# The beginning of an attention layer: where the context's norm, K's rotation and four scalings stand

## The chip, the cores and the metric

The kernel runs on one core of one Trainium2 chip. The metric is device time in microseconds (us). The program computes a whole two-layer model, and its time is that of one execution.

## The reference, cut to what matters

The model has a latent stream of 1024 tokens, a context of 256 tokens, and a width of 1024. Each layer first normalises and modulates its input, and then mixes. What is touched here is the first part of the first layer, the attention layer:

```
shift, scale, gate = adaln(c, w_ada[0], b_ada[0])              # latent; the context has its own three
u  = rms_normalize(h)  * (1 + scale[:, None]) + shift[:, None]
uc = rms_normalize(hc) * (1 + scale_c) + shift_c
q, k, v, g = split(u @ w_in)       # q 1024, k 256, v 256, g 1024 columns; the same for uc
q, k = axial_rope(q, row, col), axial_rope(k, row, col)        # the latent tokens' alone
...
y = (o * silu(g)) @ w_out
```

## The kernel before, in words

The tokens lie in three tiles, `TT = [(0, 512), (512, 512), (1024, 256)]`: tile 0 and tile 1 are the latent tokens, tile 2 is the context. A tile's activations are held transposed, as eight pieces of 128 features by 512 (or 256) tokens, with an index k of 0 to 7. Every fp32 product is made of three products of rounded halves: a value x is split in a high part (`uH` for activations, `wh` for weights, a cast on ScalarE) and a low part (`uL`, `wl`, the difference, on VectorE or GpSimd), and `mm3` issues high by high (L248 of before), and the two mixed products (L249, L250).

`norm0` prepares the input. For tile 0 it sums the squares, computes the modulation's vectors (`ada0`, from the weights `w_ada`), and has the inner function `modulate(e)`, which does the half e of the eight pieces: it scales and shifts a piece in place (the tile named `uL`, since it lies in the buffer that tile 1's low part takes later), casts it to `uH`, and subtracts for the low part. For e = 0 the scaling is one `tensor_scalar` on VectorE (L469), for e = 1 it is one `activation` on ScalarE (L471). Beside it run four projections of the gate (`half(e, x)`, x from 0 to 3), whose results are taken up by `g_out`: a tanh on ScalarE (L567), a multiplication on VectorE (L568), and a store. Then, in one loop, tiles 1 and 2 are normalised: `stats(i)` squares the rows on ScalarE (L442) and gives the factor per token (`rr`), and `modulate(0, h, r, i, k)` scales a piece on VectorE (L309), casts it on ScalarE (L310) and makes the low part on VectorE (L311). The context's pieces are the tiles `xc`.

`qkvg` then projects. `kproj(x, i)` makes two heads of K for tile i: 24 matrix products into one accumulator, then, for i < 2, the rotation `rope` (multiplication by the cosine L527 and a shuffle `STREAM_SHUFFLE` L528 on VectorE, which are the last two readers of the accumulator, multiplication by the sine on GpSimd L529, an addition on VectorE L530), a cast (L548) and the low part `kL` (L549), a store to DRAM and copies back into `kHH`, issued by GpSimd. `vproj(b)` makes V for 128 tokens: 24 matrix products into an accumulator, a cast (L602), and the low part `v` on VectorE (L603), the last reader of the accumulator. The order of tile 0 is `kproj(0, 0)`, four `vproj`, `kproj(1, 0)`; then tile 1, then tile 2, then Q and the rest of the gate.

The accumulators of all these are tiles of one name, `pj`, of which there are four: a projection can begin when the fourth one before it has been read out. Matters of order: every engine runs its own queue in order. The queues' order comes from a scheduling layer, which follows the order of the code where dependencies and its own estimate leave it, and which `issue_after(x)` tells to hold what is written inside until after instruction x. Memory of a closed pool is taken again by later tiles, which then wait for the last users.

Of the kernel before, what the change touches and what calls it, by code (L numbers as in the profile page):

```python
# [17 lines left out]
P = 128  # L18
D = 1024
KT = D // P  # L20
LAT = 1024
# [92 lines left out]
class Kernel:  # L114
# [203 lines left out]
    def layer0(self):  # L318
        nc, t, a = self.nc, self.t, self.a
        cps = ExitStack()  # L320
        BUFS.update(S=1, pj=4, wr=7, qf=2, ql=2, wh=4, wl=4, sqt=2)
        self.psA = self.pool("psA", space=PSUM, ctx=cps)
        NB = (LAT + CTX) // P
        self.uH, self.uL = [None] * 3, [None] * 3
        cw = ExitStack()
        wvp = self.pool("wv", ctx=cw)

        self.wp = self.pool("wq", ctx=cw)
        self.pq = self.pool("qf", ctx=cw)
# [4 lines left out]
        c0 = ExitStack()  # L334
        self.q_d = [[t(self.dr, [4, 2, HD, n], F32, f"q{j}_{i}") for i, (_, n) in enumerate(TT)] for j in range(KV)]
        self.sg_d = [[t(self.dr, [2, P, n], F32, f"sg{j}_{i}") for i, (_, n) in enumerate(TT)] for j in range(KV)]
        wk, wv = self.norm0(c0, p, wvp)
        c0.close()
        ckv = ExitStack()
        kvp = self.pool("kv", ctx=ckv, side="right")  # L340
        self.kHH = [t(kvp, [P, LAT + CTX], F32R, f"kHH{j}") for j in range(KV)]
# [5 lines left out]
        self.qkvg(p, wk, wv, wvp)  # L347
# [48 lines left out]
        self.modulation(0, n, row, ps)  # L396
        return mm, self.last_mod

    def norm0(self, c0, p, wvp):


        nc, t, a = self.nc, self.t, self.a
        ps = self.psA
        p1 = self.p0 = self.pool("n0", ctx=c0, side="right")
        hs, nat, raws = {}, {}, {}


        xc = [t(p1, [P, KT // 2, CTX], F32, "xc", 2) for _ in range(2)]

        def load_x(i):  # L410

# [25 lines left out]

        def stats(i):

            ss = t(p1, [P, 4], F32, "ss", 2)  # L440
            for b, x in enumerate(nat[i]):
                nc.scalar.activation(x, x, AF.Square, accum_out=ss[:, b : b + 1])  # L442
            return self.rstd_n(p1, ss, TT[i][1], D)
# [10 lines left out]
        acc = t(p1, [P, 512], F32, "sqa")  # L454
        nc.scalar.activation(acc, hs[0][0], AF.Square)
        for k in range(1, KT):
            sq = t(p1, [P, 512], F32, "sqt")
            nc.scalar.activation(sq, hs[0][k], AF.Square)
            nc.vector.tensor_tensor(acc, acc, sq, op=ALU.add)
        r = self.rstd_c(p1, acc, 512, D)  # L460
        self.alloc_u(0)
        m = self.mod[0]
        pj = [t(ps, [P, 512], F32, "pj") for _ in range(G0)]
# [1 line left out]
        def modulate(e):  # L465
            for k in range(4 * e, 4 * e + 4):
                h, uh = hs[0][k], self.uH[0][:, k, :]
                if e == 0:
                    nc.vector.tensor_scalar(out=h, in0=h, scalar1=m[:, 8 + k, 0:1], scalar2=m[:, k, 0:1], op0=ALU.mult, op1=ALU.add)  # L469
                else:  # L470
                    nc.scalar.activation(h, h, AF.Identity, bias=m[:, k, 0:1], scale=m[:, 8 + k, 0:1])  # L471
                nc.scalar.copy(uh, h)  # L472
                nc.vector.tensor_sub(self.uL[0][:, k, :], h, uh)

# [36 lines left out]
        modulate(1)  # L511
        for x in range(G0):
            half(1, x)
            self.g_out(p if x < 2 else p1, pj[x], x, 0, "qf" if x < 2 else "gq")
        for i in (1, 2):
            r = stats(i)
            self.alloc_u(i)
            for k in range(KT):
                self.modulate(0, hs[i][k], r, i, k)
        return wk, wv  # L520

    def rope(self, pool, ps, i, out):
        nc = self.nc
        s, n = TT[i]
        b = self.t(pool, [P, 512], F32, "rope_b")
        s -= self.rope_o
        nc.vector.tensor_mul(out, ps, self.cos[:, s : s + n])  # L527
        nc.vector.stream_shuffle(b, ps, mask=[(j + 16) % 32 for j in range(32)])  # L528
        nc.gpsimd.tensor_tensor(b, b, self.sin[:, s : s + n], op=ALU.mult)  # L529
        nc.vector.tensor_add(out, out, b)  # L530

# [42 lines left out]
    def g_step(self, p, w, x, i):  # L574
        self.g_out(p, self.proj_h(self.psA, w, self.uH, self.uL, i), x, i)

    def qkvg(self, p, wk, wv, wvp):
# [9 lines left out]
        def kproj(x, i):  # L587
            s, n = TT[i]
            h, _ = self.qk(p, self.proj_h(ps, wk[x], self.uH, self.uL, i), i, self.kL[x][:, s : s + n])
            nc.sync.dma_start(kh_d[x][i], h.bitcast(F32))  # L590
            for e in range(2):
                for hf in range(2):
                    nc.gpsimd.dma_start(self.kHH[2 * x + e][hf * HD : (hf + 1) * HD, s : s + n], kh_d[x][i][e * HD : (e + 1) * HD, :])

        def vproj(b):
            i = 0 if b < 4 else (1 if b < 8 else 2)
            o = (b * P) - TT[i][0]
            pj = t(ps, [P, 512], F32, "pj")
            self.mm3(pj[:, :256], [(self.uH[i][:, k, o : o + P], self.uL[i][:, k, o : o + P],
                                    wv[k // 2][0][:, k % 2, :], wv[k // 2][1][:, k % 2, :]) for k in range(KT)])  # L600
            pv = pj[:, :256].rearrange("p (j d) -> p j d", j=KV)
            nc.scalar.copy(v[:, b, :, :HD], pv)  # L602
            nc.vector.tensor_sub(v[:, b, :, HD:], pv, v[:, b, :, :HD])  # L603
# [1104 lines left out]
```

## Time and profile before

| | |
|---|---|
| runs before | 1789.54, 1794.72, 1792.93 us; median 1792.93 |
| profiled execution | 1788.45 us, of which the span of the trace is 1786.8 us |
| instructions | 28991 |
| busy | TensorE (PE) 97%, VectorE (DVE) 67%, ScalarE (ACT) 49%, GpSimd (POOL) 45% |

A profile line gives, for an instruction or a run of like ones, its start in us from the start of the span, its length, its engine, the line of the code, the operation, what it writes and reads, and how many; in square brackets stands the time for which the engine stood idle before it, and what released it. PEld is TensorE's loading of weights, which overlaps the products. PEclk is the clock that TensorE was granted, as a share of the full one.

### The profile page before, as it was taken

Reading aid. Unit: us, or ns where it says so; the run is one execution under the profiler, and the core shown is the slowest. Engines: PE = TensorE matmul, PEld = TensorE weight load, DVE = VectorE, ACT = ScalarE, POOL = GpSimd, SP = SyncE. Lnnn points to the kernel's source line nnn. Section 1 sums busy time; section 2 is a strip of 40 time slices with the busy share of each in tenths; the row PEclk is TensorE's granted clock in tenths of the full one; section 3 lists DMA queues with packets and bytes.
Section 4 is the critical chain, followed back from the end, with each engine's and each line's share of the span. In section 5 each row is a group of like instructions: output and inputs, shape, how many; then the busy total and the mean of one; then the engine's idle time right before and its main releaser. Section 6 shows DMA issues by size and latency. Waiting matters only on the chain.

```text
span 1786.8 us, 28991 instructions
## 1 busy us (share of the span) xinstructions
PE 1733.4 (97%) x10319; PEld 1493.5 (84%) x10319; DVE 1197.2 (67%) x2115; ACT 874.4 (49%) x1906; POOL 799.0 (45%) x1068
## 2 busy tenths in 40 slices
PE   6899999999999999999999999999999999999997
PEld 2697788888888877778898898989889898988887
DVE  4634436778877885685776858677685867876634
ACT  3612227777777774452444534444453444544522
POOL 2431127555575555103555463736446363554321
PEclk9999999999999999999999999999999999999998
DMA  9658866444554536212323323232332322555533
GB/s 346 221 147 267 280 183 152 111 96 106 114 152 129 130 101 221 86 53 74 80 69 89 84 74 93 72 85 75 90 85 72 91 77 81 180 166 167 182 103 114
DMA packets 211931, 227.61 MB, mean 127 GB/s; under 512 B 15820, under 2 KB 149068, under 8 KB 211788
## 3 DMA queue, kind: packets, MB, share of 16 engines
q1 hardware_dynamic: 177724, 207.12, 38.8%
q0 software_dynamic: 34064, 18.65, 5.7%
q8 instruction: 81, 1.33, 0.3%
q14 instruction: 62, 0.51, 0.1%
HBM read 190.88 MB, written 35.13 MB: 126 GB/s over the span
## 4 chain that ended last, share of the span: by engine, by line
PE 84%; DVE 9%; issue 2%; ACT 2%; DMA 2%; POOL 0%; SPq 0%; DVEq 0%; ACTq 0%; POOLq 0%
PE pj L1106 18%; PE pj L1140 10%; PE pj L1541 7%; PE pj L248 7%; PE pj L249 6%; PE pj L250 6%; PE psD L1091 4%; PE psX L1293 3%; PE pt L686 3%; PE psD L1209 2%; PE pv L693 2%; PE psX L1262 2%; PE psX L1261 2%; PE pv L692 2%; PE S L661 1%
## 5 line engine op out<-in xcount | busy, mean ns | idle before, releaser
L248 PE MATMUL pj<-uH,wh 128*128 128x512 f32 (+1 forms) x712 | 257.3, 363 | 6.3 <-ACT uH L472 3.7
L249 PE MATMUL pj<-uL,wh 128*128 128x512 f32 (+1 forms) x712 | 243.3, 342 | 0.5 <-POOL uL L709 0.4
L250 PE MATMUL pj<-uH,wl 128*128 128x512 f32 (+1 forms) x712 | 242.4, 341 | 1.3 <-POOL wl L233 1.1
L1106 PE MATMUL pj<-uH,wh 128*128 128x512 f32 x512 | 173.6, 411 | 1.2 <-ACT bn L1061 1.2
L1106 PE MATMUL pj<-uH,wl 128*128 128x512 f32 x512 | 170.2, 403 | 0.0
L1106 PE MATMUL pj<-uL,wh 128*128 128x512 f32 x512 | 168.1, 402 | 0.0
L1184 POOL TENSOR_TENSOR xw<-xn,dtdec 128x256 f32<-128x256 f32 x144 | 95.9, 667 | 159.8 <-PE psD L1209 75.7
L248 PEld LDWEIGHTS pj<-uH,wh 128*128 128x128 f32 x712 | 135.6, 191 | 34.0 <-issue 6.3
L250 PEld LDWEIGHTS pj<-uH,wl 128*128 128x128 f32 x712 | 135.0, 190 | 18.5 <-POOL wl L233 2.1
L1140 PE MATMUL pj<-wh,uH 128*128 128x256 f32 x512 | 150.4, 294 | 0.0
L1140 PE MATMUL pj<-wl,uH 128*128 128x256 f32 x512 | 150.2, 293 | 0.0
L1140 PE MATMUL pj<-wh,uL 128*128 128x256 f32 x512 | 149.9, 293 | 0.0
L249 PEld LDWEIGHTS pj<-uL,wh 128*128 128x128 f32 x712 | 135.8, 191 | 16.1 <-issue 3.0
L691 DVE TENSOR_TENSOR pl<-pt,ph 128x512 fp32r<-128x512 f32 x168 | 114.1, 688 | 47.2 <-ACT ph L690 46.0
L233 POOL TENSOR_TENSOR wl<-wr,wh 128x512 fp32r<-128x512 f32 x76 | 99.6, 1315 | 85.4 <-ACT wh L231 84.5
L665 DVE CUSTOM_DVE_ANT_0 sm<-S,mask,nsink 128x640 f32<-128x640 f32 (+2 forms) x160 | 119.2, 772 | 19.7 <-PE S L661 12.6
L1325 ACT ACTIVATE uT<-psX,nw 128x128 f32<-128x128 f32 x128 | 46.6, 364 | 171.6 <-PE psX L1324 170.7
L667 ACT ACTIVATE sm<-sm,nm 128x640 f32<-128x640 f32 (+2 forms) x160 | 118.7, 742 | 16.7 <-DVE nm L665 16.1
L690 ACT CAST ph<-pt 128x512 fp32r<-128x512 f32 x168 | 97.5, 585 | 55.8 <-PE pt L686 51.8
L231 ACT CAST wh<-wr 128x512 fp32r<-128x512 f32 (+1 forms) x116 | 74.7, 648 | 87.0 <-PE pj L249 67.1
L1106 PEld LDWEIGHTS pj<-uH,wl 128*128 128x128 f32 x512 | 95.8, 188 | 20.0
L1106 PEld LDWEIGHTS pj<-uL,wh 128*128 128x128 f32 x512 | 95.3, 188 | 19.3
(342 smaller groups left out, 4861.9 us busy)
## 6 DMA issues: line engine op xcount, KB each, us to landing
wr<-w_x SPq DMA_DIRECT2D x32, 512.0 KB, 4.2
M<-acs SPq DMA_DIRECT2D x64, 256.0 KB, 5.3
bw<-acs SPq DMA_DIRECT2D x64, 256.0 KB, 5.7
wr<-w_sk SPq DMA_DIRECT2D x24, 512.0 KB, 4.5
wr<-wg SPq DMA_DIRECT2D x40, 256.0 KB, 4.3
qs<-q POOLq DMA_DIRECT2D x40, 256.0 KB, 3.9
wada<-w_ada SPq DMA_DIRECT2D x16, 512.0 KB, 8.1
wr<-wq SPq DMA_DIRECT2D x32, 256.0 KB, 2.9
```

The source lines that it names most:

```text
L233: (eng or nc.vector).tensor_tensor(l, raw, h, op=ALU.subtract)
L248: self.nc.tensor.matmul(ps, lh, rh, start=first and i == 0, stop=False)
L249: self.nc.tensor.matmul(ps, lh, rl, start=False, stop=False)
L250: self.last_mm = self.nc.tensor.matmul(ps, ll, rh, start=False, stop=last and i == n - 1)
L665: nc.vector.tensor_tensor_reduce(out=sm[:, :W], in0=Sv, in1=self.mask[:, m0 : m0 + W], scale=-SCALE, scalar=self.nsink[:, 4 * j + r : 4 * ...
L667: nc.scalar.activation(sm[:, :W], sm[:, :W], AF.Exp, bias=nm[:, r : r + 1], scale=-1.0, accum_out=sums[:, r : r + 1])
L690: nc.scalar.copy(ph, ptf)
L691: nc.vector.tensor_sub(pl, ptf, ph)
L1106: self.pe = nc.tensor.matmul(raw[:, 512 * i : 512 * i + 512], l[:, k, :], r[i][:, k, :], start=k + y == 0, stop=k == KT - 1 and y == 2)
L1140: self.pe = nc.tensor.matmul(pj[:, c], l, r[:, k, :], start=c % 2 + q + k + y == 0, stop=c % 2 == 1 and q == 1 and k == 3 and y == 2)
L1184: nc.gpsimd.tensor_tensor(xw, X(st, c).rearrange("p (r h) -> p r h", r=R), self.dtdec[:, c, hd(d, g)].unsqueeze(2).broadcast_to([P, R, HP] ...
L1541: self.pe = nc.tensor.matmul(banks[x], l[:, z, sl], r, start=k == 2 * qs[0] and y == 0, stop=k == 2 * qs[-1] + 1 and y == 2)
```

## The change

Four things are changed.

- `norm0` ends after the first half (k = 0 to 3) of tile 1. The other half, and all of tile 2, become a function `late`, which `qkvg` calls: the second half of tile 1 is issued after the shuffle of `kproj(0, 0)`, and tile 2's norm after the last V of tile 0 has been read out.
- `modulate(1)` scales on VectorE, as `modulate(0)` does.
- The fourth gate result of tile 0 (x = 3) goes into a tile of its own, `sqa`, in the place of the third one's `gq`.
- The memory is rearranged for this: the context's tiles are in a pool `n1` that stays open longer, and K's `kHH` is allocated after that pool is closed, so that tile 0's copies into `kHH` (`spread`) are issued then.

```
@@ norm0
-                if e == 0:
-                    nc.vector.tensor_scalar(out=h, in0=h, scalar1=m[:, 8 + k, 0:1], scalar2=m[:, k, 0:1], op0=ALU.mult, op1=ALU.add)
-                else:
-                    nc.scalar.activation(h, h, AF.Identity, bias=m[:, k, 0:1], scale=m[:, 8 + k, 0:1])
+                nc.vector.tensor_scalar(out=h, in0=h, scalar1=m[:, 8 + k, 0:1], scalar2=m[:, k, 0:1], op0=ALU.mult, op1=ALU.add)
...
-            self.g_out(p if x < 2 else p1, pj[x], x, 0, "qf" if x < 2 else "gq")
-        for i in (1, 2):
-            r = stats(i)
-            self.alloc_u(i)
-            for k in range(KT):
-                self.modulate(0, hs[i][k], r, i, k)
-        return wk, wv
+            self.g_out(p if x < 2 else p1, pj[x], x, 0, "qf" if x < 2 else ("gq", "sqa")[x - 2])
+        rs = {}
+
+        def late(i, ks):
+            if i not in rs:
+                rs[i] = stats(i)
+                self.alloc_u(i)
+            for k in ks:
+                self.modulate(0, hs[i][k], rs[i], i, k)
+
+        late(1, range(4))
+        return wk, wv, late
@@ qkvg
-        for i, (s, n) in enumerate(TT):
+        kproj(0, 0)
+        with self.tc.issue_after(self.turned.ins):
+            late(1, range(4, KT))
+        for b in range(4):
+            low = vproj(b)
+        kproj(1, 0)
+        with self.tc.issue_after(low.ins):
+            late(2, range(KT))
+        keys()
+        for x in range(2):
+            spread(x, 0)
+        for i, (s, n) in list(enumerate(TT))[1:]:
             kproj(0, i)
-            if i:
-                kproj(1, i)
+            kproj(1, i)
             for b in range(s // P, (s + n) // P):
                 vproj(b)
-            if i == 0:
-                kproj(1, i)
```

Here `self.turned` is the shuffle that `rope` issued last, `keys()` closes the pool `n1` and allocates `kHH`, and `spread(x, i)` is the four copies into `kHH` that stood in `kproj`.

What the rewriting does to the queues is seen at two places. The first is ScalarE's queue at `modulate(1)`, tile 0's second half. Before, the scalings (L471, on the tile `uL`) stand between casts of weights (`wh`) and ahead of the four casts to `uH`:

```order
L231 CAST wh_144_442<-wvr_143_440 128x512
L471 ACTIVATE uL1_65_164<-uL1_65_164,mod0_5_74 128x512 x2
L231 CAST wh_147_448<-wvr_146_446 128x512
L471 ACTIVATE uL1_65_164<-uL1_65_164,mod0_5_74 128x512 x2
L231 CAST wh_150_454<-wvr_149_452 128x512
L472 CAST uH0_99_244<-uL1_65_164 128x512 x2
L231 CAST wh_135_424<-wr_134_422 128x512
L472 CAST uH0_99_244<-uL1_65_164 128x512
```

Now, in the same place of ScalarE's queue:

```order
L231 CAST wh_144_445<-wvr_143_443 128x512
L231 CAST wh_147_451<-wvr_146_449 128x512
L475 CAST uH0_99_247<-uL1_65_167 128x512
L231 CAST wh_150_457<-wvr_149_455 128x512
L475 CAST uH0_99_247<-uL1_65_167 128x512 x3
L231 CAST wh_135_427<-wr_134_425 128x512
```

And on VectorE, where the scalings (L474 now) stand between the modulation's vector (`mod`) and the four subtractions (L476):

```order
L223 TENSOR_SCALAR mod0_5_74<-mod0_5_74 128x8
L474 TENSOR_SCALAR uL1_65_167<-uL1_65_167,mod0_5_74 128x512 x4
L476 TENSOR_TENSOR uL0_100_248<-uL1_65_167,uH0_99_247 128x512 x4
L385 TENSOR_TENSOR sqt_177_585<-ident_1_63,rc_176_582 128x512
L576 SCALAR_TENSOR_TENSOR qf_171_525<-qf_171_525,pj_101_249 128x512
```

Four scalings have left ScalarE's queue, the first cast to `uH` waits for one scaling in the place of four, and VectorE has all four scalings ahead of the first subtraction.

The second place is VectorE's queue at the accumulators of tile 0: the norm of tile 1 (L309 and L311 on `uH2`, `uL2`, the loaded halves), K's rotation (`rope_b`), the norm of tile 2 (`xc`), the fourth gate (`gq_174`, reading `pj_104`), and the four V (`v`). Before:

```order
L309 SCALAR_TENSOR_TENSOR uL2_166_485<-uL2_166_485,mod0_5_74,rr512_179_586 128x512 x4
L311 SCALAR_TENSOR_TENSOR uL1_181_589<-uH2_165_484,mod0_5_74,uH1_180_588 128x512 x4
L380 TENSOR_TENSOR sqt_184_620<-ident_1_63,rc_183_617 128x256
L311 SCALAR_TENSOR_TENSOR uL1_181_589<-uL2_166_485,mod0_5_74,uH1_180_588 128x512 x4
L527 TENSOR_TENSOR qf_206_700<-pj_205_675,cos_167_488 128x512
L528 STREAM_SHUFFLE rope_b_208_702<-pj_205_675 128x512
L309 SCALAR_TENSOR_TENSOR xc_61_160<-xc_61_160,mod0_5_74,rr512_186_624 128x256 x4
L309 SCALAR_TENSOR_TENSOR xc_62_161<-xc_62_161,mod0_5_74,rr512_186_624 128x256 x4
L568 SCALAR_TENSOR_TENSOR gq_174_570<-gq_174_570,pj_104_249 128x512
```

After (the fourth gate is `sqa_174`):

```order
L576 SCALAR_TENSOR_TENSOR sqa_174_573<-sqa_174_573,pj_104_252 128x512
L309 SCALAR_TENSOR_TENSOR uH2_165_487<-uH2_165_487,mod0_5_74,rr512_179_589 128x512 x4
L311 SCALAR_TENSOR_TENSOR uL1_181_592<-uH2_165_487,mod0_5_74,uH1_180_591 128x512 x4
L535 TENSOR_TENSOR qf_195_649<-pj_194_624,cos_167_491 128x512
L536 STREAM_SHUFFLE rope_b_197_651<-pj_194_624 128x512
L309 SCALAR_TENSOR_TENSOR uL2_166_488<-uL2_166_488,mod0_5_74,rr512_179_589 128x512 x4
L538 TENSOR_TENSOR qf_195_649<-qf_195_649,rope_b_197_651 128x512
L311 SCALAR_TENSOR_TENSOR uL1_181_592<-uL2_166_488,mod0_5_74,uH1_180_591 128x512 x3
L616 TENSOR_TENSOR v_182_609<-pj_198_671,v_182_609 128x4x64
L616 TENSOR_TENSOR v_182_609<-pj_199_698,v_182_609 128x4x64
```

The readers of the accumulators (the fourth gate, the cosine and the shuffle of K, the low parts of V) now stand ahead of the context's norm, and K's first two readers stand ahead of tile 1's second half; the rotation's addition (L538), which waits for GpSimd, stands ahead of the low parts of V.

More of the change, by code (lines that the diff above doesn't have):

```diff
@@ L346, in layer0, with keys @@
         self.sink = t(kvp, [P, HEADS], F32, "sink")
-        self.qkvg(p, wk, wv, wvp)
+        def keys():
+            c2.close()
+            kh = self.pool("kvh", ctx=ckv, side="right")
+            self.kHH = [t(kh, [P, LAT + CTX], F32R, f"kHH{j}") for j in range(KV)]
+        self.qkvg(p, wk, wv, wvp, late, keys)
         if "u" in self.dump:
@@ L404, in norm0 @@
         p1 = self.p0 = self.pool("n0", ctx=c0, side="right")
+        p2 = self.pool("n1", ctx=c2)
         hs, nat, raws = {}, {}, {}
[L408 removed]
+        xc = [t(p2, [P, KT // 2, CTX], F32, "xc", 2) for _ in range(2)]
         def load_x(i):
@@ L527, in rope @@
         nc.vector.tensor_mul(out, ps, self.cos[:, s : s + n])
-        nc.vector.stream_shuffle(b, ps, mask=[(j + 16) % 32 for j in range(32)])
+        self.turned = nc.vector.stream_shuffle(b, ps, mask=[(j + 16) % 32 for j in range(32)])
         nc.gpsimd.tensor_tensor(b, b, self.sin[:, s : s + n], op=ALU.mult)
@@ L575, in g_step, with qkvg @@
         self.g_out(p, self.proj_h(self.psA, w, self.uH, self.uL, i), x, i)
-    def qkvg(self, p, wk, wv, wvp):
+    def qkvg(self, p, wk, wv, wvp, late, keys):
         nc, t, a = self.nc, self.t, self.a
@@ L590, in kproj, with spread @@
             nc.sync.dma_start(kh_d[x][i], h.bitcast(F32))
+            if i:
+                spread(x, i)
+        def spread(x, i):
+            s, n = TT[i]
             for e in range(2):
```

17 lines of the change are left out of this document (8 added, 9 removed).

## The prediction

> **What bounds the kernel now.** I read, in this order, TensorE's (PE's) waits in the stretch around the change, its timeline there, the windows for its clock, and then the queues of the engines it waits for. The waits between 20 and 140 us (engine and line, released by what, total us, times, longest):
>
> ```profile
> PE pj L248 <- ACT uH L472: 3.7, 2, 2.8
> PE pj L248 <- DVE rope_b L528: 2.3, 1, 2.3
> PE pj L248 <- DVE gq L568: 1.6, 1, 1.6
> PE pj L248 <- DVE v L603: 1.6, 1, 1.6
> ```
>
> The first line is the cast of tile 0's second half (its longest case, 2.8; the other lies ahead of the change). The others are the four accumulators `pj`: PE stands because VectorE (DVE) has not yet read one out. PE's timeline shows where these stand in the work:
>
> ```profile
> 52.02 1.65 PE L248 MATMUL pj<-uH,wh 128*128 128x512 f32 x3 [2.77 <-ACT uH L472]
> 53.47 0.73 PE L249 MATMUL pj<-uL,wh 128*128 128x512 f32 x1
> ...
> 55.24 0.39 PE L250 MATMUL pj<-uH,wl 128*128 128x512 f32 x1
> ...
> 65.05 0.79 PE L248 MATMUL pj<-uH,wh 128*128 128x512 f32 x1
> ...
> 70.93 0.28 PE L248 MATMUL pj<-wh,uH 128*128 128x256 f32 x1
> ...
> 77.13 0.28 PE L250 MATMUL pj<-wh,uL 128*128 128x256 f32 x1
> 79.74 0.39 PE L248 MATMUL pj<-wh,uH 128*128 128x256 f32 x1 [2.34 <-DVE rope_b L528]
> ...
> 82.60 0.28 PE L250 MATMUL pj<-wh,uL 128*128 128x256 f32 x1
> 84.51 0.39 PE L248 MATMUL pj<-wh,uH 128*128 128x256 f32 x1 [1.63 <-DVE gq L568]
> ...
> 87.37 0.28 PE L250 MATMUL pj<-wh,uL 128*128 128x256 f32 x1
> 89.22 0.50 PE L248 MATMUL pj<-uH,wh 128*128 128x512 f32 x1 [1.57 <-DVE v L603]
> ```
>
> K's first projection runs from 65.05, the four V from 70.93, K's second head pair begins at 89.22, and two V's first products and that of K are late. Windows of PE's work and clock (us, then per engine busy time and count, then PEclk, the share of the DMA engines, GB/s):
>
> ```profile
> 48.40:51.80 3.40, 0.85 (x4) 0.38 (x2) 0.00 (x0) 3.40 (x6) 1.82 (x3) 1.00 1.04 406
> 51.80:55.20 3.40, 3.18 (x7) 2.34 (x8) 3.20 (x3) 3.40 (x8) 2.41 (x2) 0.50 1.04 418
> 82.50:85.90 3.40, 1.77 (x15) 1.56 (x14) 3.40 (x9) 2.33 (x6) 0.00 (x0) 1.00 0.17 64
> 85.90:89.30 3.40, 1.83 (x16) 1.63 (x14) 3.40 (x9) 1.41 (x5) 1.38 (x3) 1.00 0.52 106
> 89.30:250.00 160.70, 160.70 (x1015) 131.16 (x1016) 64.01 (x120) 37.22 (x72) 33.27 (x40) 1.00 0.73 229
> ```
>
> The last row matters most: from 89.3 to 250 us PE is busy for all of 160.70 us, at full clock. What the change takes from the front is therefore passed on, unless it makes a wait of its own.
>
> **First part: the scalings on VectorE.** Before, the vector `mod` is ready and ScalarE (ACT) scales in two pairs, with casts of weights between:
>
> ```profile
> 46.62 0.84 DVE L223 TENSOR_SCALAR mod<-mod 128x8 f32<-128x8 f32 x1
> 47.49 1.52 ACT L471 ACTIVATE uL<-uL,mod 128x512 f32<-128x512 f32 x2 [0.91 <-DVE mod L223]
> ...
> 49.43 1.51 ACT L471 ACTIVATE uL<-uL,mod 128x512 f32<-128x512 f32 x2
> ```
>
> PE stands for 2.77 us, then does its three high products, then needs the first low part, at 53.47. Now VectorE scales four times, then subtracts. The nearest rows are those of the first half, which already goes that way, beside GpSimd (POOL) making low parts of weights (the line of a source line's view gives nanoseconds, lowest, median, highest):
>
> ```profile
> L469 DVE TENSOR_SCALAR uL<-uL,mod x4: 535/1466/1491, 25.6 to 29.8; 128x512 f32<-128x512 f32 x4
> 25.57 4.72 DVE L469 TENSOR_SCALAR uL<-uL,mod 128x512 f32<-128x512 f32 x4
> 30.21 2.48 DVE L473 TENSOR_TENSOR uL<-uL,uH 128x512 fp32r<-128x512 f32 x4
> 23.27 6.28 POOL L233 TENSOR_TENSOR wl<-wr,wh 128x512 fp32r<-128x512 f32 x4 [6.45 <-ACT wh L231]
> ```
>
> The scaling that falls behind POOL's last operation takes 535 ns, those beside POOL 1466: VectorE waits for POOL. POOL has such low parts to make in the second half too (1.82 us of them in the window from 48.40). I take the whole 4.72: 47.49 + 4.72 = 52.21 for the end of the scalings, and a quarter of 2.48, 0.62, for the first subtraction: 52.8. The first cast to `uH` comes after one scaling, 1.47, so PE does its three high products near 49.6 and then waits again. At 52.8 it needs the low part: 0.6 us earlier than 53.47. VectorE's time is not hidden here; it is what PE waits for. What ScalarE loses, four times about 0.75, was on this path before and is now off it.
>
> The rest of this term is the clock. After the gap the window 51.80 to 55.20 has a clock of 0.50, and from 53.47 to 55.24 four products take 1.77 us; at the pace of K's first projection (65.05 to 70.93, 24 products in 5.88, 0.245 each) they would take 1.0. PE was busy for 0.85 of 3.4 us in the window whose gap cost it the clock, and 1.77 and 1.83 of 3.4 in two that kept it. The change puts three products, some 0.8 us, into the gap: 1.65 of 3.4, nearer to those that kept it. With full clock the gain is 0.6 + 0.8 = 1.4, with the same drop 0.6. I take 1.0, between the two, since the windows' phase need not be that of this execution.
>
> The Trainium skill, "TensorE: Matmul & The Clock Gate", section "Why this matters for your kernels", says that matmul bursts should have no gaps over about 3 us between them, or the clock goes to half. The trace differs a little: a gap of 2.77 us was enough. By that rule both of the change's shorter gaps leave the clock full and the term is 1.4 in the place of 1.0.
>
> Bounds of this term: above, the 535 ns for all four scalings, 47.49 + 2.14 + 0.62 = 50.3, so 3.2 earlier, and 0.8 for the clock: a gain of 4.0. Below, 1491 for each, and for the first subtraction the 1774 that a two-input VectorE operation takes at most beside POOL (row L311 below): 47.49 + 5.96 + 1.77 = 55.2, a loss of 1.8. I stay at 1.0, since the row of 4.72 is the same operation with the same neighbour.
>
> **Second part: who reads the accumulators first.** Rows of VectorE before:
>
> ```profile
> 78.36 0.68 DVE L527 TENSOR_TENSOR qf<-pj,cos 128x512 f32<-128x512 f32 x1
> ...
> 78.97 0.71 DVE L528 STREAM_SHUFFLE rope_b<-pj 128x512 f32<-128x512 f32 x1
> 79.59 4.27 DVE L309 SCALAR_TENSOR_TENSOR xc<-xc,mod,rr 128x256 f32<-128x256 f32 x8
> 83.78 0.67 DVE L568 SCALAR_TENSOR_TENSOR gq<-gq,pj 128x512 f32<-128x512 f32 x1
> ...
> 88.76 1.07 DVE L603 TENSOR_TENSOR v<-pj,v 128x256 fp32r<-128x256 f32 x3
> ```
>
> K's accumulator is full at 70.93 and read at 78.36, behind all of tile 1's norm; the fourth gate's is full before 65.05 and read at 83.78, behind eight scalings of the context; V's low parts come at 88.76, behind the rest of the context. The three stalls, from the end of the last product at its pace of 0.12 to the next start, are 79.74 - 77.25 = 2.49, 84.51 - 82.72 = 1.79, and 89.22 - 87.49 = 1.73: 6.0 us. Where do the readers come now? For this I need
>
> ```profile
> 66.27 2.85 DVE L309 SCALAR_TENSOR_TENSOR uH<-uH,mod,rr 128x512 f32<-128x512 f32 x4 [1.89 <-ACT rr L384]
> 71.69 2.73 DVE L311 SCALAR_TENSOR_TENSOR uL<-uH,mod,uH 128x512 fp32r<-128x512 f32 x4
> L311 DVE SCALAR_TENSOR_TENSOR uL<-uL,mod,uH x4: 737/739/1774, 74.7 to 77.7; 128x512 fp32r<-128x512 f32 x4
> 73.32 0.60 ACT L231 CAST wh<-wvr 128x512 fp32r<-128x512 f32 x1
> 74.00 1.90 POOL L233 TENSOR_TENSOR wl<-wvr,wh 128x512 fp32r<-128x512 f32 x1 [2.34 <-ACT wh L231]
> 79.77 1.44 POOL L529 TENSOR_TENSOR rope_b<-rope_b,sin 128x512 f32<-128x512 f32 x1 [3.86 <-DVE rope_b L528]
> ```
>
> The fourth gate is read right after its tanh, ahead of the row at 66.27: no wait. Tile 1's first half: scaling from 66.27 to 69.1, low parts to 71.8, K's cosine and shuffle to 73.2. The accumulator that K leaves is wanted by the fourth V, near 79: cover of 6 us. The next one needed is that of the first V, by K's second head pair. On PE that is due at 65.05 + 5.88 + 96 products of 0.12 = 82.4. On VectorE: four scalings of the second half, 2.85, to 76.0, and 1.03 for one of them caught by POOL (1774 less 739), 77.0. Then the addition, which waits for the product with the sine. That stands on POOL behind the low part of the last quarter of V's weights, whose cast ACT reaches no later than before, 73.32, since it has four pieces fewer ahead: 73.9, two POOL operations of 1.90 and 1.44, 77.3 (77.5 with the small power operation in the way). Addition 0.68, three low parts 2.2, V's low part 0.36: 80.7. So 1.7 us of cover are left, and if POOL or VectorE is later than that by more, each us costs one. All of tile 1's `uL` is there by 82, and wanted 5.9 after 82.4.
>
> The context's norm, now begun only after K's second pair's shuffle near 89, needs 4.27 for scaling and 2.85 or more for low parts, beside the 23 us that PE has in two K of tile 1 (5.88 each) and four V (2.9 each): it is hidden, and so are tile 0's copies into `kHH`, first read in the attention. GpSimd issues them ahead of tile 1's products with the sine and waits there for the context's last low part, near 97 (89 + 4.27 + 2.85 and a wait or two); what stands behind those products on VectorE are V's low parts of tile 1, whose accumulators PE wants no earlier than its context projections, near 111 (82.4 + 3 times 5.88 + 4 times 2.9). The gate's store in SP's queue passes two loads of Q's weights, which PE wants after all of that. I cost these at nothing.
>
> **The sum.** 6.0 + 1.0 = 7.0 us. Against the profiled execution of 1788.45 that is 1781.4; this execution is 4.5 below the median of the runs, so for the median I subtract from that: 1792.93 - 7.0 = 1785.9. About 0.3%, 5.4 us, is what a measurement of this kernel can tell from no change, so the forecast stands 1.6 us beyond that.
>
> **The rivals.** First, a part is lost: the scalings go by their lower bound (a loss of 1.8 in the place of a gain of 1.0), or the addition is later than its cover and K's second pair waits as long. For it speaks that every VectorE operation met by POOL is stretched (1466 for 535, 1774 for 739); against it, that the cover counts one such meeting already. 6.0 - 1.8 = 4.2, so 1788.7. The Trainium skill, "SBUF — State Buffer", section "SBUF: two separate sides", has the port pair of VectorE and GpSimd as an exclusive lock for a whole instruction; the trace agrees with 535 against 1466, and it is the rule that speaks against putting scalings there.
>
> Second, the 7 us are given back, because a later stretch is set by something else, such as the transfers of Q's weights. For it: the DMA share of 0.73 up to 250. Against it: PE waits there for nothing. 1792.9.
>
> Third, it gets slower. The last quarter of V's weights is loaded late, and now the rotation's addition, and behind it V's low parts, stand in VectorE's queue behind what POOL makes of it, while PE's third and fourth V want it too.
>
> ```profile
> 57.21 0.37 SPq L501 DMA_DIRECT2D wvr<-wv x1
> ...
> DMA to landing us min/median/max: 7.4/7.4/7.4
> ```
>
> Issued at 57.21 behind loads that wait for buffers which POOL frees, it lands near 64.6; its low part (2.5 us later) is wanted by PE near 77.2, so a landing after 74.7 costs each us, and from 81.7 all gain is gone. POOL delayed by scalings could hold SP's queue. Three more landing times, 22 us, would put it at 86.8: 12.1 lost, 1785.9 + 12.1 = 1798.0, 5.1 slower than before. Against it stand 10 us of cover.
>
> **How the numbers follow.** Forecast 0.68, first rival 0.17, second 0.09, third 0.06. The runs shown spread over 5.2 us, so of the forecast some 0.85 is measured beyond 5.4 us, of the first rival 0.3: 0.58 + 0.05 = 0.63 for faster. Slower by over 0.3%: half of the third, and some scatter of the second, 0.06. The rest, 0.31, is the same. Range: the second part alone with the lower bound gives 1788.7, and scatter of 2.8 on it 1791.5; the sum with the first term's upper bound, 10.0, gives 1782.9, and 2.4 of scatter 1780.5. This leaves out most of the second and all of the third rival.
>
> **What would show it.** Right: PE without a wait between K's first projection and 250 us, K's second pair beginning near 81.4, the first subtraction of the second half ending near 52.8, PEclk 1.00 after it. Wrong: a wait of PE for the low part of V or the shuffle (cover too small), scalings that end after 53.5, or a span shorter by 7 us at 250 and not at its end.

## The result, and the profile after

The changed kernel takes 1786.11 us (median of 5 runs, 1783.91 to 1788.02) against 1792.93 for the kernel before, run beside it; the ratio is 0.9964, with an interval of 0.9947 to 0.998. The forecast was 1785.9. The total came out; two of its terms did not, and they made up for each other, so that the match is in part luck.

The profiled execution after took 1788.02 us, with a span of 1786.0. That of before took 1788.45, with 1786.8. So these two traces differ by 0.8 us only, where the medians differ by 6.8: the trace of before is of an execution 4.5 below its median, that of after of one 1.9 above. What the change did has to be read stretch by stretch.

TensorE's waits between 20 and 250 us, after (line, released by what, total us, times, longest):

```profile
PE pj L248 <- ACT uH L475: 4.0, 2, 3.6
PE pj L249 <- DVE uL L476: 2.4, 2, 2.3
PE aps L197 <- DMA wl<-w_ada: 1.3, 1, 1.3
PE pt L219 <- ACT arow L400: 0.7, 1, 0.7
```

The three waits for readers of accumulators (`rope_b`, `gq`, `v`) are gone. One of 1.3 for a transfer of `w_ada` has come, far behind the change (near 223 us); it is not the change's alone, as the kernel before with a warm-up (below) has it too, 1.3. PE's timeline, after:

```profile
52.17 0.96 PE L248 MATMUL pj<-uH,wh 128*128 128x512 f32 x3 [0.41 <-ACT uH L475]
55.40 0.80 PE L249 MATMUL pj<-uL,wh 128*128 128x512 f32 x1 [2.27 <-DVE uL L476]
55.99 0.63 PE L250 MATMUL pj<-uH,wl 128*128 128x512 f32 x1
...
68.50 1.02 PE L387 MATMUL pt<-sqt,ones 128*128 128x512 f32 x2
...
86.38 0.40 PE L248 MATMUL pj<-uH,wh 128*128 128x512 f32 x1
```

The gap of 2.77 has become 0.41 and 2.27. At 86.38 K's second head pair begins, at once behind the fourth V. VectorE's and GpSimd's rows, after:

```profile
49.12 0.84 DVE L223 TENSOR_SCALAR mod<-mod 128x8 f32<-128x8 f32 x1
49.99 4.75 DVE L474 TENSOR_SCALAR uL<-uL,mod 128x512 f32<-128x512 f32 x4
54.66 3.57 DVE L476 TENSOR_TENSOR uL<-uL,uH 128x512 fp32r<-128x512 f32 x4
82.12 0.68 DVE L538 TENSOR_TENSOR qf<-qf,rope_b 128x512 f32<-128x512 f32 x1
84.71 0.74 DVE L616 TENSOR_TENSOR v<-pj,v 128x256 fp32r<-128x256 f32 x2
49.88 4.12 POOL L233 TENSOR_TENSOR wl<-wvr,wh 128x512 fp32r<-128x512 f32 x3
78.57 1.75 POOL L537 TENSOR_TENSOR rope_b<-rope_b,sin 128x512 f32<-128x512 f32 x1
101.73 4.19 POOL L606 DMA_DIRECT2D kHH<-k  x8 [6.74 <-DVE uL L311]
```

The scalings took 4.75, as row L469 of before had it (4.72), beside three low parts on GpSimd. And the windows (columns as in the prediction):

```profile
50.80:54.20 3.40, 1.92 (x8) 0.92 (x6) 3.40 (x3) 1.76 (x3) 3.09 (x3) 1.00 1.06 414
54.20:57.60 3.40, 2.20 (x5) 1.82 (x6) 3.40 (x6) 3.28 (x6) 1.54 (x1) 0.54 1.04 419
57.60:61.00 3.40, 3.40 (x9) 2.63 (x9) 0.64 (x1) 2.85 (x7) 0.53 (x2) 0.50 1.04 388
89.30:250.00 160.70, 159.35 (x1010) 129.99 (x1010) 70.08 (x132) 40.93 (x81) 34.72 (x41) 1.00 0.73 228
```

The clock fell to a half for two windows (read in finer steps: from 54.5 to 61.3 us), where before it fell for one (51.8 to 55.2). From the two timelines, stretch by stretch (after against before, us):

| stretch | before | after | difference |
|---|---|---|---|
| start to the end of the second L223 (`mod`) | 47.46 | 49.96 | +2.5 |
| from there to the first low-part product (L249) | 6.01 | 5.44 | -0.6 |
| from there to the norm's product `pt` of tile 1 | 11.12 | 13.10 | +2.0 |
| from there to K's second head pair | 24.63 | 17.88 | -6.75 |
| from there to the end | 1697.6 | 1699.6 | +2.0 |

The fourth row is the second part of the change, and it gives more than its 6.0. The first row stands ahead of every instruction that the change touches; the third is the clock. Below, "the front" is the first row, and "the stretch of the scalings" is the second and third together.

### The profile page after: what moved, and what is told of

It is laid out like the page before. It is cut to its first block, busy times and chain, and to the rows that moved or that the text cites. A ratio compares the mean times of both kernels' runs of the same rounds, so it can differ in the third digit from the quotient of the medians.

```text
span 1786.0 us, 28989 instructions
## 1 busy us (share of the span) xinstructions
PE 1735.7 (97%) x10319; PEld 1495.7 (84%) x10319; DVE 1202.1 (67%) x2119; ACT 873.2 (49%) x1902; POOL 799.6 (45%) x1068
## 4 chain that ended last, share of the span: by engine, by line
PE 84%; DVE 8%; DMA 3%; issue 2%; ACT 2%; POOL 1%; SPq 0%; DVEq 0%; ACTq 0%; POOLq 0%
PE pj L1127 18%; PE pj L1161 10%; PE pj L1562 7%; PE pj L248 7%; PE pj L249 7%; PE pj L250 6%; PE psD L1112 4%; PE psX L1314 3%; PE pt L707 3%; PE psD L1230 2%; PE pv L714 2%; PE psX L1283 2%; PE psX L1282 2%; PE pv L713 1%; PE S L681 1%
## 5 line engine op out<-in xcount | busy, mean ns | idle before, releaser
L249 PE MATMUL pj<-uL,wh 128*128 128x512 f32 (+1 forms) x712 | 244.5, 344 | 2.8 <-DVE uL L476 2.4
L249 PEld LDWEIGHTS pj<-uL,wh 128*128 128x128 f32 x712 | 136.2, 191 | 18.4 <-DVE uL L476 4.6
L712 DVE TENSOR_TENSOR pl<-pt,ph 128x512 fp32r<-128x512 f32 x168 | 114.2, 689 | 47.2 <-ACT ph L711 46.0
```

The costliest lines, as they stand in the source:

```text
L249: self.nc.tensor.matmul(ps, lh, rl, start=False, stop=False)
L712: nc.vector.tensor_sub(pl, ptf, ph)
```

## The experiments

Each was run in several rounds beside the kernel before. All runs of the kernel before in these sets, 78 of them, have a median of 1793.1 and lie between 1787.9 and 1798.3. Where I pool runs, I give the difference of the means with a 95% interval from resampling the runs.

**The changed kernel again**, unaltered:

> The changed kernel once more, for a second trace. If the readers' order is the cause, the stretch from the norm's second-last matmul (L387, 68.50 in the first trace) to K's second pair is 17.9 us again (24.6 before), and the time is 1784 to 1788. If the half clock after the gap is an accident of its phase, the stretch from the end of the modulation's vector (L223) to L387, 18.5 in the first trace and 17.1 before, comes out near 16 to 17; if it belongs to the change, 18 or more again. If the wait for a load of w_ada near 222 us (1.35) belongs to the change, it is there again with 1 to 2 us; else it is gone.

1786.01 us (9 runs), ratio 0.9964, 0.9949 to 0.9978; span 1784.3. The front ended at 50.6, the stretch of the scalings took 17.3 (18.5 in the trace above, 17.1 in that of before), and `pt` to K's second pair 17.88 to the hundredth. The clock was at half for 3.41 us here, half as long as in the trace above. The wait for `w_ada` was there again, 1.7.

**Each part alone.** First the readers' order without the scalings:

```
 # the changed kernel, with the scalings as before
+                if e == 0:
                     nc.vector.tensor_scalar(out=h, in0=h, ...)
+                else:
+                    nc.scalar.activation(h, h, AF.Identity, bias=m[:, k, 0:1], scale=m[:, 8 + k, 0:1])
```

> The changed kernel with the scalings of tile 0's second half back on ScalarE. Readers' order as the only cause: 17.9 us from L387's place to K's second pair, and a time as the changed kernel's, 1784 to 1788. Scalings worth 1.0 as the prediction has it: 1 us longer from L223 to the norm's matmul than the changed kernel at the same clock. Scalings worth the whole or a large part: 1789 or more.

1783.12 us (6 runs), ratio 0.9954, 0.9937 to 0.997. Then the scalings alone, in the kernel before:

```
 # the kernel before
-                if e == 0:
                     nc.vector.tensor_scalar(out=h, in0=h, ...)
-                else:
-                    nc.scalar.activation(h, h, AF.Identity, ...)
```

> The kernel before with nothing changed but the scalings of tile 0's second half, now on VectorE. Readers' order as the cause: the three waits for accumulators stay (5.5 us of waits, 24.6 us in that stretch), and the time is 1791 to 1794. Scalings as the cause: 1789 or less.

1795.33 us (12 runs), ratio 1.0014, 1.0001 to 1.0028. The first is 2.9 us faster than the whole change, the second 2.2 slower than before: putting the scalings on VectorE costs time both ways. In the second trace I found a wait that is this kernel's own; of its waits from 20 to 250 us:

```profile
PE pj L248 <- ACT uH L469: 6.1, 2, 5.7
PE pt L382 <- DVE sqt L380: 4.1, 1, 4.1
PE pj L248 <- DVE rope_b L525: 2.4, 1, 2.4
PE pj L249 <- DVE uL L470: 2.3, 1, 2.3
```

The context's norm is now late (4.1), because its squares on ScalarE now stand behind the casts of tile 1; that wait isn't in the changed kernel. `pt` to K's second pair took 28.28 there, against 24.63, and behind that wait and the one for `rope_b` the clock was at half for 3.41 us each (from 83.8 and 90.6), which the trace of before doesn't have. The runs agree: their mean granted clock is 0.9908, that of the 78 runs of before 0.9925.

**How much of the order matters.** All of tile 1's norm ahead of K's rotation, only the context's behind the V:

```
 # the changed kernel
-        late(1, range(4))
+        late(1, range(KT))
...
-        with self.tc.issue_after(self.turned.ins):
-            late(1, range(4, KT))
```

> The changed kernel, but with the whole norm of tile 1 ahead of K's rotation, as before; only the context's norm is late. From the rows, K's accumulator is then read out near 79.7 on the prediction's scale, and the fourth V wants it at 79.6: a wait of 0 to 0.8 us, so the context's place is nearly the whole gain, 18 to 18.7 us in that stretch and 1784 to 1789. If the rotation amid tile 1's scaling matters as much as the context, a wait of 2 us or more at the fourth V and 20 us or more.

1789.75 us (12 runs), ratio 0.998, 0.9967 to 0.9993. `pt` to K's second pair takes 19.56, with waits of 0.7 for `v` and 0.6 for `rope_b`: between the two cases that I had named. So moving the context, with the gate's own tile, gives 5.1 of the 6.75 and K's rotation amid tile 1's scalings the other 1.7. In the means of the runs (14 of the changed kernel) the rotation's place is worth 3.4, interval 1.5 to 5.3.

**The gate's own tile alone**, in the kernel before:

```
-            self.g_out(p if x < 2 else p1, pj[x], x, 0, "qf" if x < 2 else "gq")
+            self.g_out(p if x < 2 else p1, pj[x], x, 0, "qf" if x < 2 else ("gq", "sqa")[x - 2])
```

> The kernel before with one part of the change alone: the fourth gate result in its own tile, so that its multiplication is done on VectorE ahead of tile 1's norm. Theory A (the order of the readers on VectorE's queue is what costs; three readers stand behind the norm): the fourth gate's stall (1.6) goes, but VectorE's queue ends where it did, so the wait of K's second pair for V's low part grows by about as much; K's second pair comes 0.5 to 1 us earlier, the time falls by as much. Theory B (each stall counts by itself): 1.6 to 1.8 us earlier and faster.

1794.06 us (12 runs), ratio 1.0011, 0.9997 to 1.0024: no gain in time. The trace shows where the stall went; of the waits from 20 to 250 us:

```profile
PE pj L248 <- DVE v L603: 5.6, 1, 5.6
```

Before, three stalls of 2.3, 1.6 and 1.6 stood there, 5.5 together. Now there is a single one as long. `pt` to K's second pair is 24.06, 0.6 less than before, as the first theory had it. All three accumulators wait for one queue on VectorE; freeing one of them only makes PE arrive earlier at the next. The forecast fall of the time did not come, and this trace shows where it can go: behind the stall in one piece the clock was at half from 91.3 to 98.1, which the three short stalls did not bring in the trace of before. This is why the order had to be changed as a whole.

**Is the late front the scalings' doing?** In the first six traces (before, the change twice, each part alone, the context alone; the gate's tile was run later) those with the scalings on VectorE had their front at 50.0 to 51.6, and both with them on ScalarE at 47.5 and 47.6, although ahead of it all engines' rows stand in the same order. PE's first products, of `w_ada` (L398 of after) and of the sum of squares (`pt`), ran at different paces:

```profile
14.36 1.05 PE L365 MATMUL pt<-ones,sqa 128*128 128x1 f32 x8
```

in before, and in after

```profile
14.24 1.87 PE L370 MATMUL pt<-ones,sqa 128*128 128x1 f32 x8
16.04 3.63 PE L398 MATMUL aps<-wada,cs 128*32 128x512 f32 x12
```

To take this away, 24 products of a constant went ahead of PE's first real one, in three kernels: before, the change, and the change with ScalarE's scalings. Nothing else moves on any engine:

```
+    def warm(self, n):
+        d = self.t(self.psA, [P, 512], F32, "pj")
+        for x in range(n):
+            self.nc.tensor.matmul(d[:, :128], self.ones, self.ones[:, :128], start=True, stop=True)
...
+        self.warm(16)
...
-        nc.scalar.activation(acc, hs[0][0], AF.Square)
+        sq0 = nc.scalar.activation(acc, hs[0][0], AF.Square)
+        with self.tc.issue_after(sq0.ins):
+            self.warm(8)
```

> The kernel before, with 24 products of a constant tile on TensorE ahead of its first real one (16 at the start, 8 behind the first square at about 7.8 us), whose result nobody reads; every other row of every engine stands as before. In the traces so far the products of w_ada, TensorE's first, start at 11.07 to 11.54 us and run at half pace (about 0.4 us each) for 3 to 8 us: the norm's eight products behind them took 1.05 in two traces (before, and after with the scalings on ScalarE), 1.34 in two and 1.87 in two (the four with the scalings on VectorE), and the second L223 ended at 47.5 in the first two, at 50 to 51.6 in the others. Theory A: that is chance of the execution (when TensorE gets to full pace), not the scalings. Then the warm-up puts it at full pace at 11.1 in every kernel: the norm's products take 1.05 or less, L223 ends at 47.5 or up to 1.5 earlier, and the time falls on the low end of the runs of before or below it, 1785 to 1789, with less scatter. Theory B: the scalings on VectorE make the front late in another way; then before's median stays near 1793, since its front was early already in its trace.

> The changed kernel with the same 24 products ahead. Theory A (the late front is chance of TensorE's pace): L223 ends within 0.7 us of where it ends in the two other kernels with the warm-up, and the time is 6 to 7 us below before with the warm-up: 1779 to 1782. Theory B (VectorE's scalings cost it the front): L223 still ends 2 to 4 us later than in the other two, and the time is 2 to 3 us above that with the scalings on ScalarE.

> The changed kernel with the second half's scalings back on ScalarE, and the same 24 products ahead. Theory A: the same front as the changed kernel with the warm-up, the first low-part product 0.6 us later behind L223, and a time within 1.5 us of it, either way. Theory B: 2 to 3 us below it, since its front is 2 to 4 us earlier.

Measured: 1791.75 (12 runs), 1784.1 (7) and 1783.08 (6). In all three traces the front ended early, at 47.7, 47.3 and 47.5. (In the first of them PE's first eight products were slow all the same, 3.19, so a slow start need not make the front late.) The times did not move as theory A had it: before with the warm-up is where before was (difference of means -0.05, interval -1.5 to 1.5). Both with the scalings on VectorE and on ScalarE were run once more:

> The changed kernel with the warm-up once more, beside its sister with the scalings on ScalarE, to tell what the scalings alone are worth in the whole. Theory A (they are worth their 0.6 us, and 1.3 where the clock is kept): front (second L223) near 47.5 again, a time 0.5 to 1.5 us below the sister's. Theory B (they cost, in the late front or later): 1 to 3 us above it.

> The changed kernel with the second half's scalings on ScalarE and the warm-up, once more. Theory A: front near 47.5, 17.05 us from there to the norm's products, and 0.5 to 1.5 us slower than with the scalings on VectorE. Theory B: 1 to 3 us faster.

1785.28 us (12 runs), ratio 0.9964, 0.995 to 0.9977, and 1781.93 (5 runs), ratio 0.9947, 0.9927 to 0.9966. The fronts were the opposite of theory B, 47.2 with VectorE and 51.7 with ScalarE; the times, 3.4 apart, were as theory B had them, so whatever the scalings cost, these two fronts don't show it. With all traces:

| scalings on | end of the front, us, one trace each |
|---|---|
| ScalarE | 47.5, 47.6, 47.7, 47.5, 51.7, and 52.1 (the gate's tile alone) |
| VectorE | 50.0, 50.6, 51.6, 50.5, 47.3, 47.2, and 46.9, 47.6 (the two below) |

So the scalings neither make the front late nor keep it early: four of six and four of eight are early. I take it for chance of an execution, and my first impression from six traces was wrong; fourteen traces can't exclude that the scalings make a late front somewhat likelier. One thing that it hangs on is seen in the second trace with ScalarE and the warm-up, its timeline (L404 is `w_ada`, L376 the sum) and a window:

```profile
11.40 3.20 PE L404 MATMUL aps<-wada,cs 128*32 128x512 f32 x8 [2.62 <-DMA wada<-w_ada]
14.53 1.87 PE L376 MATMUL pt<-ones,sqa 128*128 128x1 f32 x8
```

```profile
12.40:15.80 3.40, 3.27 (x12) 1.46 (x11) 1.39 (x3) 0.63 (x1) 0.00 (x0) 0.50 1.05 387
```

Its warm-up had ended 2.62 us earlier, and PE was at half clock again. With the scalings on VectorE and the warm-up, the gap was shorter:

```profile
11.11 1.05 PE L404 MATMUL aps<-wada,cs 128*32 128x512 f32 x4 [1.51 <-DMA wada<-w_ada]
...
13.77 1.05 PE L376 MATMUL pt<-ones,sqa 128*128 128x1 f32 x8 [0.34 <-DVE sqa L473]
```

A slow pace there is one contribution. The other is that VectorE's second four multiplications by `rr` take 4.63 in five of the six late fronts, in the place of 2.49 in all early ones; GpSimd's first low parts run beside them. Nor can one trace's span be read as its front: with ScalarE's scalings and the warm-up, a front 4.2 later ended in a span only 0.6 longer (1780.6 against 1780.0).

**Is it GpSimd that makes the scalings dear?** Three of the four low parts of V's weights, which GpSimd makes beside the scalings, go to VectorE, behind the four subtractions. No other row moves on any engine. With the warm-up, and without it:

```
 # the changed kernel; vh is the cast (ScalarE), raw the loaded quarter
-            for q in range(4):
-                ...
-                wv.append(self.split_w(raw, [P, 2, 256], nc.gpsimd, wvp))
+            for q in range(3):
+                raw, ld = load_v(q)
+                vh = t(wvp, [P, 2, 256], F32R, "wh")
+                nc.scalar.copy(vh, raw)
+                rawv.append((raw, vh))
...
         modulate(1)   # its last subtraction is self.low
+        with self.tc.issue_after(self.low.ins):
+            for raw, vh in rawv:
+                vl = t(wvp, [P, 2, 256], F32R, "wl")
+                nc.vector.tensor_tensor(vl, raw, vh, op=ALU.subtract)
+                wv.append((vh, vl))
+        with last():
+            wv.append(self.split_w(load_v(3)[0], [P, 2, 256], nc.gpsimd, wvp))
```

> The changed kernel with the warm-up, and three of the four low parts of V's weights made by VectorE, behind the four subtractions of tile 0's second half, in the place of GpSimd beside the scalings; no other row of any engine moves. Theory A (the scalings take 4.75 us because GpSimd holds VectorE off, so the term of the scalings was set by its lower row): without GpSimd a scaling takes its 535 ns or so, the four 2.1 to 2.9 in the place of 4.75, the first product with a low part comes 2.9 to 3.5 us behind the second L223 in the place of 5.45, the norm's products of tile 1 2 us earlier behind it (13.8 in the place of 15.8 with the clock kept), and the time falls by 1 to 2 us against the changed kernel with the warm-up. Theory B (the scalings are as slow by themselves, or what is won ahead of 65 us is taken back by the loads): 4.7 again, or a time within 0.7 us of it.

> The changed kernel without any warm-up, with the low parts of three of the four quarters of V's weights made by VectorE behind tile 0's subtractions, so that GpSimd does nothing beside the scalings. With the warm-up this edit took 4.5 us (means of 6 and of 19 runs, interval 2.3 to 7.1), the scalings took 1.92 and TensorE did not wait. Theory A (GpSimd beside the scalings is what made them dear, whatever the front does): the four scalings take 1.9 again, TensorE waits for no uL nor uH of the second half, the stretch from the second L223 to tile 1's norm product is near 13.0 and not 15.8 to 18.5, and the time is 1780 to 1783, 3 to 6 below the changed kernel (median 1786.0 of 14). Theory B (the gain was of that kernel's chance, or needs the warm-up): within 1.5 us of the changed kernel.

With the warm-up 1781.99 us (6 runs), ratio 0.9941, 0.9921 to 0.9961. Without it 1780.06 (6 runs, 1778.7 to 1784.71), ratio 0.9934, 0.9914 to 0.9954. This is the fastest version, and it beats both kernels of the case. Against the changed kernel the difference of the means is 4.8 us without the warm-up (interval 2.8 to 6.7) and 4.5 with it (2.3 to 7.1). Against the versions with ScalarE's scalings it is 2.3 (12 runs against 17, interval 0.5 to 4.0). The timeline without the warm-up:

```profile
46.76 0.83 DVE L223 TENSOR_SCALAR mod<-mod 128x8 f32<-128x8 f32 x1
47.63 1.92 DVE L474 TENSOR_SCALAR uL<-uL,mod 128x512 f32<-128x512 f32 x4
49.47 2.49 DVE L476 TENSOR_TENSOR uL<-uL,uH 128x512 fp32r<-128x512 f32 x4
51.87 1.88 DVE L526 TENSOR_TENSOR wl<-wvr,wh 128x512 fp32r<-128x512 f32 x3
49.23 0.84 PE L248 MATMUL pj<-uH,wh 128*128 128x512 f32 x3
50.20 0.50 PE L249 MATMUL pj<-uL,wh 128*128 128x512 f32 x1
```

Its windows:

```profile
47.60:51.00 3.40, 3.27 (x14) 2.36 (x13) 3.37 (x7) 2.79 (x6) 0.00 (x0) 1.00 1.05 408
51.00:54.40 3.40, 3.40 (x16) 2.82 (x15) 2.76 (x5) 3.40 (x7) 2.89 (x1) 1.00 1.04 418
```

The four scalings take 1.92 in the place of 4.75, GpSimd is idle in the first window, PE stands for no more than 0.2 us at the second half of tile 0, and the clock stays at 1.00. From L223 to the norm's product `pt` are 12.95 us, where the changed kernel needed 18.5, 17.3, 15.8 and 15.8 in its four traces.

## Why the prediction was right, and where it was wrong

**The second part** was right in its mechanism: readers first, no stall left. Of the cover of 1.7 us, 1.3 was left: V's first low part is read out by 85.1 (84.71 and half of 0.74), PE needs it at 86.38, and the addition ended at 82.8. The context's norm and the copies into `kHH` were hidden, as costed; GpSimd's wait there ended at 101.73, not near 97, since all of it stands 4 us later in this trace, and PE waited for nothing of it. Its size was put at 6.0; the stretch gave 6.75 in the trace, 0.5 of which is the context's `pt` product, which moved behind it. In the means of the runs it is more: the change with the scalings on ScalarE, with and without warm-up (17 runs), is 9.7 us below before (78), interval 8.3 to 10.9. From K's second pair to the end the four traces in the order of before (warm-up, scalings alone and gate tile among them) took 1699.6 on average, the three with readers first and ScalarE's scalings 1696.2. Why, when a single trace differs by up to 4 from the next of its kind, stays open. A candidate is the clock: three of the four traces in the order of before have it at half for 3.41 or 6.8 us in or behind the stalls (from 79.7, from 83.8 and 90.6, from 91.3), and none of the ten others. That it makes up the difference is not shown.

**The first part** had the wrong sign in the runs: the step that failed is "I take 1.0, between the two", and with it the assumption that what is won in the stretch of the scalings is won at the end. The earlier low part was worth 0.57, as forecast (0.6). For the clock I let it be kept (0.8) or be lost as before (0); it can also be lost for longer. With the gap split, it was at half for two windows of 3.41 us in one trace with the scalings on VectorE (18.5 in the place of 17.1), for one in three (17.3, 17.1, 17.3) and not at all in two (15.8 twice). The six traces with ScalarE's scalings all lost it for one (17.1 to 17.5). So in the traces this stretch is 0.2 shorter on average with VectorE (17.0 against 17.2), and not 1.0. The rule of the Trainium skill ("TensorE: Matmul & The Clock Gate", "Why this matters for your kernels": no gaps over about 3 us) doesn't separate these cases, since the gaps are 0.41 and 2.27 in traces of either kind.

What separates them is where the gap falls on a raster. Read in steps of 0.2 us, the clock's falls up to 1760 us last 3.41 us or a multiple of it in every trace, and within a trace their starts lie multiples of 3.413 apart (before: 24.47 and 51.78, eight times that). Against the program the raster lies elsewhere in each trace. On it, PE's work in the windows around the gap (the quiet kernel apart, which has no such gap):

| trace | window, us | PE busy, us of 3.41 | clock in the next window |
|---|---|---|---|
| before | 48.37 to 51.78 | 0.88 | 0.50 |
| after | 51.09 to 54.50 | 1.63 | 0.50 |
| after | 54.50 to 57.91 (at 0.50) | 2.51 | 0.50 |
| after, again | 52.61 to 56.03 | 0.96 | 0.50 |
| after, warm-up | 48.08 to 51.49, and 51.49 to 54.90 | 2.00, and 2.14 | 1.00, and 1.00 |

In all traces between 47 and 100 us, the clock fell behind each full-clock window with at most 1.63 us of work and behind none with 1.74 or more. So the prediction's way of counting (0.85 lost it, 1.77 kept it) was right; its 1.65 lies at that edge. It saw, too, that the phase may differ, but priced the doubt by the middle of two values.

By the runs the scalings on VectorE cost 2.4 us in the changed kernel (33 runs against 17, interval 1.0 to 3.8) and 2.6 in the kernel before (12 against 78, interval 1.1 to 4.0). For the kernel before the trace shows where: the wait of 4.1 for the context's norm, and the clock behind it. For the changed kernel it doesn't. The stretch of the scalings isn't longer on average, and the mean granted clock of the runs is the same within the noise (0.9925 against 0.9926). From K's second pair to the end its four traces take 1698.7 on average against 1696.2 for three; of that, the wait for `w_ada` near 223 (1.3 to 1.8, against none, 1.6 and 0.5) is about 1 us, and it comes in other kernels too. The cause of the 2.4 in the changed kernel stays open.

**Why the scalings take long** was named rightly in the rival "a part is lost": a VectorE operation beside GpSimd is stretched. The source line of the eight scalings (lowest, median and highest ns) after, and then in the quiet version without the warm-up, where only the first half has GpSimd beside it:

```profile
L474 DVE TENSOR_SCALAR uL<-uL,mod x8: 533/1474/1499, 27.9 to 54.2; 128x512 f32<-128x512 f32 x8
```

```profile
L474 DVE TENSOR_SCALAR uL<-uL,mod x8: 534/546/1494, 25.6 to 49.0; 128x512 f32<-128x512 f32 x8
```

The upper bound of the term in the prediction (all four at 535, a gain of 3.2 and 0.8 for the clock) is what the quiet version reaches in this stretch: 12.95 against 17.13 is 4.2. What is shown is that GpSimd beside the scalings makes them dear and that taking it away wins 4.5 to 4.8 us; that the 2.4 of the move itself is this price is not shown. The Trainium skill's rule of an exclusive lock between VectorE and GpSimd ("SBUF — State Buffer", "SBUF: two separate sides") agrees with both rows.

**The rivals.** The first one, "a part is lost", came true in its first half: by the runs the scalings lose 2.4, more than its lower bound of 1.8; the larger second part hid it. The late load of V's last quarter did not come: PE waits for it in no trace. Giving back later may have come in a small way, as the wait for `w_ada` of 1.3, which the kernel before with the warm-up has as well. Of the signs named, K's second pair near 81.4 came at 86.38 in this trace, later above all by 2.5 for the front and 2.0 for the clock; with the early front and the clock kept it came at 80.98 and 80.85. The scalings ended at 54.74 and not before 53.5, a sign of being wrong, but only because the front was 2.5 later: from `mod` on they took 4.78 us, where 4.72 was forecast. The full clock behind the gap did not hold, the absence of waits up to 250 us held but for that one, and "a span shorter by 7 at 250 and not at its end" is not what happened: the trace's span is shorter by 0.8 in all, since the front (+2.5), the clock (+2.0) and the part behind K's second pair (+2.0) go against the 6.75.

So the total of 7.0 was right by two errors of opposite sign, which is luck: by the runs, 9.7 for the second part (6.0 forecast) and -2.4 for the first (+1.0 forecast).

## What to carry to other kernels

When several accumulators are read by one engine, put all the readers ahead of the bulk work on its queue together: freeing one only moves the stall to the next. Before moving an operation to VectorE, look at what GpSimd does beside it; giving VectorE the neighbour's work as well was worth twice what the move had cost. And before reading a difference between two traces as an effect, look at how far the same unchanged stretch wanders between traces of like kernels: here the front alone wandered by 5 us, most of the effect.

## What the runs showed of the hardware that was not expected

- PE idle for 1.44, 1.51, 1.56 and 1.90 us between the warm-up and its first real products kept these at four in 1.05 us; idle for 2.51 and 2.62 put them at eight in 3.2, with a granted clock of 0.50 in a window of one. In some traces without a warm-up the same slow pace stands beside a PEclk of 1.00.
- The clock falls and rises on a raster of 3.41 us, whose place against the program differs from execution to execution. The same split gap (0.41 and 2.27, with three products of 0.96 between) cost two half-clock windows in one trace, one in three and none in two; one gap of 2.77 cost one in the trace of before.
- Four multiplications on VectorE, beside GpSimd's first low parts near 24 us, take 2.49 or 4.63. The order and the starts don't fix which: with GpSimd starting 0.77 us behind VectorE, both happened.
